# Output projection of a hybrid layer: conv half as seven block products, quarter-wide weight scales, sums held in PSUM

## The chip, the cores and the metric

One core of a Trainium2 chip runs the kernel. Its engines work side by side, each through its own instruction stream in order: TensorE (PE) multiplies into PSUM, VectorE (DVE) and ScalarE (ACT) read PSUM and SBUF, GpSimd (POOL) works on SBUF, and SyncE's queue (SP) issues most DMA transfers. The metric is the device time of one execution in microseconds; the result is given as the median of repeated runs. TensorE's clock has two levels, 1.2 and 2.4 GHz; the profile shows what share of full speed was granted.

## The reference, cut to what matters

For 512 tokens of width 2048 the layer computes an SSD group and a conv group, joins them to a row of 4096 and projects that row back:

```python
mixed = jnp.concatenate([y_ssd, y_conv], axis=-1)            # (1, 512, 4096)
h = h + jnp.einsum('ble,ed->bld', mixed, w_out)              # w_out (4096, 2048), float32
return rmsnorm(h, final_norm_w)
```

`y_conv = silu(layernorm(conv31(glu))) * silu(cg)` is the half that the change computes in another way. All inputs and the output are float32.

## The kernel before, in words

**Numbers.** Each float32 operand is scaled by a power of two and split into two float16 parts, hi and lo. A product is three matmuls (hi by hi, hi by lo, lo by hi; `mm`, line 388). A weight tile of 128x2048 floats (1 MB, buffer `raw`, three of them) is prepared by `prepare` (line 406): ACT squares it with a running sum, a 1-column matmul on PE adds that sum over the partitions into one column of the PSUM tile `pk` (`total`, line 366), DVE and POOL make the scale and its inverse from the exponent (`scales`, line 373), ACT writes hi (`w_h`, four buffers), DVE writes lo (`w_l`, three buffers; `low`, line 385).

**Items.** `plan` (line 1028) lists 121 items in the order in which PE takes them: 73 of the input projection with the SSD and the 31-tap convolution behind them, 16 for the gate `cg` (`take_cg`, line 893), and 32 of the output projection. The layer norm's sums over the channels (`center`, line 870, and `normalize`, line 885) hang on two items of the last SSD groups. An output item is a quarter `d` of the 2048 output columns (512 wide) by a block `p` of 512 of the 4096 inputs: `p` 0 to 3 is the SSD half (`mixh`, `mixl`), 4 to 7 the conv half (`z`, `y` or `cc`). It takes 4 token tiles of 128 x 4 input tiles of 128 x 3 = 48 matmuls with 512 moving columns (`project_out`, line 929, `out_tile`, line 942). After every item DVE adds its four PSUM tiles, scaled, to the result rows in SBUF (`take_out`, line 987; the rows are called `big`, as they lie where the layer's input was, and start with `x`). The conv half is split into hi and lo by `split_conv` (line 912) in the gate stage, with a scale for each block of 512 channels. The last three items of the last quarter are taken token tile by token tile, so that a row can be finished and stored while the next is multiplied (`project_last`, line 948; `finish`, line 1011).

**Order.** Nothing is issued in the order in which it is written. `Program` records every instruction with a cost from a small table (`Engine.cost`, line 249), gives it a due time from PE's order and simulates the engines (`times`, line 179, `AHEAD_NS` = 4000 early for what feeds the main matmuls); each engine then gets its stream in the simulated order. The 1-column matmuls are taken as soon as the simulation has their input. On the chip each stream is fixed: an instruction that waits holds up all behind it. All instructions carry the helper's line 284 in the profile, so groups are told apart by their tiles.

**PSUM.** Eight banks of 128x512 floats: `pp` three, `ps` three, `pst` and `pk` one each.

Of the kernel before, what the change touches and what calls it, by code (L numbers as in the profile page):

```python
# [40 lines left out]
SPLIT_AT = 2  # L41
# [5 lines left out]
N_LAST = 3  # L47
# [263 lines left out]
class Kernel:  # L311
    def __init__(self, ctx, tc, t, out):
        self.ctx, self.tc, self.t, self.out = ctx, tc, t, out
        self.program = Program()
        self.nc = Engines(self.program, tc.nc)
        self.v = self.nc.vector
        pool = self.pool
        self.const = pool("const", 1)
        self.raw = pool("raw", 3)
        self.wsp = pool("wsp", 3)  # L320
        self.big = pool("big", 1)
        self.mix = pool("mix", 1)
        self.ccp = pool("ccp", 4)
        self.wk = pool("wk", 1)
        self.tiny = pool("tiny", 4)
        self.pp = pool("pp", 3, space=PSUM)
        self.ps = pool("ps", 3, space=PSUM)
        self.pst = pool("pst", 1, space=PSUM)
        self.pk = pool("pk", 1, space=PSUM)
        self.dram = pool("dram", 1, space=DRAM)  # L330


    def pool(self, name, bufs, **kw):
        pool = self.ctx.enter_context(self.tc.tile_pool(name=name, bufs=bufs, **kw))
        return Pool(self.program, pool, name, bufs, kw.get("space") is not None)

# [29 lines left out]
    def total(self, x):  # L366

        self.n_totals += 1
        ps = self.pk_tile[:, self.n_totals - 1:self.n_totals]
        self.nc.tensor.matmul(ps, self.ones16, x.bitcast(BF16)[:, 1:2], start=True, stop=True)  # L370
        return ps

    def scales(self, m, bound=0, keep=None):


        g = self.nc.gpsimd
        e = self.small("sc_e", 1, I32)
        self.v.tensor_scalar(e, m.bitcast(I32), 1, 0x7F800000, op0=ALU.logical_shift_right, op1=ALU.bitwise_and)
        sc = self.const.tile([P, 1], I32, name=keep + "_s") if keep else self.small("sc_s", 1, I32)
        self.v.tensor_scalar(sc, e, -1.0, float((205 - bound) << 23), op0=ALU.mult, op1=ALU.add)  # L380
        inv = self.const.tile([P, 1], I32, name=keep) if keep else self.small("sc_i", 1, I32)
        g.tensor_scalar(inv, e, 1.0, float((49 + bound) << 23), op0=ALU.mult, op1=ALU.add)
        return sc.bitcast(F32), inv.bitcast(F32)
# [22 lines left out]
    def prepare(self, it, pieces=1):  # L406
        if "raw" not in it:
            self.load(it)
        his, sqs, los = [], [], []
        for k, w in enumerate(it["raw"]):  # L410
            hi = self.wsp.tile([P, 2048], F16, name="w_h", bufs=4)[:, :w.shape[1]]
            s = self.small(f"sq{k}")
            self.nc.scalar.activation(hi.bitcast(BF16), w, AF.Square, accum_out=s)
            his.append(hi)
            sqs.append(s)
        if len(sqs) > 1:
            self.nc.gpsimd.tensor_tensor(sqs[0], sqs[0], sqs[1], op=ALU.add)
        it["sc"], it["inv"] = self.scales(self.total(sqs[0]))
        for w, hi in zip(it["raw"], his):
            lo = self.wsp.tile([P, 2048], F16, name="w_l", bufs=3)[:, :w.shape[1]]  # L420
# [27 lines left out]
    def constants(self):  # L448
        nc, t, c = self.nc, self.t, self.const
        self.pk_tile, self.n_totals = self.pk.tile([P, 512], F32, name="pk"), 0  # L450
        self.ones, self.ident = (c.tile([P, P], F32, name=name) for name in ("ones", "ident"))
# [459 lines left out]

    def split_conv(self, p):
# [11 lines left out]
        nc.scalar.activation(hi, self.cc[p], AF.Copy, scale=sc)  # L924
        self.low(lo, self.cc[p], sc, hi)
        self.mixed[4 + p] = Split(hi, lo, inv)


    def project_out(self, d, p):
        def go(it):  # L930
            if d == 0 and p == 0:
                self.start_output()
            pool, name = ((self.pp, "pp"), (self.ps, "ps"))[p % 2]
            it["ps"] = []
            for i in range(TT):
                ps = pool.tile([P, S], F32, name=name) if i < 3 else self.pst.tile([P, S], F32, name="pst")
                self.out_tile(ps, it, p, i)
                it["ps"].append(ps)

        return go  # L940

    def out_tile(self, ps, it, p, i, first=0):

        m, w, n = self.mixed[p], it["parts"][0], ps.shape[1]
        at = lambda k: k * S + i * P if p >= 4 else k // 2 * TT * GC + i * GC + k % 2 * P
        self.mm(ps, [(m.cols(at(k), at(k) + P), w.cols(k * S + first, k * S + first + n)) for k in range(4)])

    def project_last(self, it):

        d, its = 3, list(enumerate(self.items))[-N_LAST:]  # L950
        its = [(x, n - len(self.items) + 8) for n, x in its]
        scs = [self.out_scale(x, p) for x, p in its]
        for i in range(TT):
            for (x, p), sc in zip(its, scs):
                parts = N_PARTS if i == TT - 1 and p == 7 else 1
                w = S // parts
                for q in range(parts):
                    pool, name = ((self.pp, "pp"), (self.ps, "ps"))[(p + q) % 2]
                    ps = pool.tile([P, S], F32, name=name)[:, :w]
                    self.out_tile(ps, x, p, i, q * w)  # L960
                    row = self.row(i)[:, d * S + q * w:d * S + (q + 1) * w]
                    self.v.scalar_tensor_tensor(row, ps, sc, row, op0=ALU.mult, op1=ALU.add)
                    if p == 7:
                        self.square(row, self.oss[:, i, d + q:d + q + 1])
            self.finish(i, parts)

    def out_scale(self, it, p):
        sc = self.small("inv0")
        self.nc.gpsimd.tensor_tensor(sc, it["inv"], self.mixed[p].inv, op=ALU.mult)
        return sc  # L970
# [15 lines left out]

    def take_out(self, d, p):
        def take(it):
            nc, v = self.nc, self.v
            ds = slice(d * S, (d + 1) * S)  # L990
            sc = self.out_scale(it, p)
            if d == 0 and p == 7:
                self.fw = self.ccp.tile([P, D], F32, name="cc")
                nc.gpsimd.dma_start(self.fw, self.t["final_norm_w"].partition_broadcast(P))
            for i in range(TT):
                row = self.row(i)[:, ds]
                v.scalar_tensor_tensor(row, it["ps"][i], sc, row, op0=ALU.mult, op1=ALU.add)
                if p == 7:
                    self.square(row, self.oss[:, i, d:d + 1])
            if d > 0 and p == 0:  # L1000
                for i in range(TT):
                    row = self.row(i)[:, (d - 1) * S:d * S]
                    v.tensor_tensor(row, row, self.fw[:, (d - 1) * S:d * S], op=ALU.mult)
            if d == 3 and p == 0:
                self.part = self.const.tile([P, TT], F32, name="part")
                v.tensor_tensor(self.part, self.oss[:, :, 0], self.oss[:, :, 1], op=ALU.add)
                v.tensor_tensor(self.part, self.part, self.oss[:, :, 2], op=ALU.add)
                v.tensor_scalar(self.part, self.part, 1.0 / D, EPS, op0=ALU.mult, op1=ALU.add)
        return take
# [18 lines left out]
    def plan(self):  # L1028
# [27 lines left out]
        for ct in range(KT):  # L1056
            add(blk(64 + ct), self.project, self.take_cg(ct))
        for p in range(4):
            self.later.append((len(items) - 13 + 4 * p + SPLIT_AT, p))
        for d in range(4):  # L1060
            for p in range(8):
                if 8 * d + p < 32 - N_LAST:
                    add([t["w_o"][d, p]], self.project_out(d, p), self.take_out(d, p))
                else:
                    add([t["w_o"][d, p]], self.project_last if p == 7 else lambda it: None)
        for i, p in self.later:
            items[i]["takes"].append(lambda it, p=p: self.split_conv(p))
        self.items = items

    def run(self):  # L1070
# [7 lines left out]
        self.conv_sums = self.const.tile([P, 4, 5], F32, name="conv_sums")  # L1078
        for i, it in enumerate(self.items):
            if i > 0:  # L1080
                self.prepare(it)
# [13 lines left out]
def _layout(inp):  # L1095
# [15 lines left out]
    lay["w_o"] = c(o.transpose(3, 0, 2, 1, 4).reshape(4, 8, P, 4 * S))  # L1111
# [30 lines left out]
```

## Time and profile before

| | |
|---|---|
| time before, median of 3 runs | 1454.96 us (1454.14 to 1455.84) |
| the profiled execution | 1456.17 us, its span 1454.4 us |
| PE busy | 1421.3 us, 98% of the span |
| DVE, ACT, POOL busy | 1131.6 us (78%), 810.3 us (56%), 213.7 us (15%) |
| the chain that ended last | PE 88%, DVE 7%, ACT 2%, DMA 1% |
| output projection on PE | about 1109 to 1444 us |

The profile is of one execution; the span is the time in which its engines had work, and 1.8 us of the execution lie around it. Busy time counts an engine as busy while any of its instructions is in flight; matmuls overlap, so a matmul that is listed with 379 ns follows the one before it by much less, and what one costs is read from the starts of neighbours in the order of time. An engine's idle time is named after what ended it. The chain of waits goes back from the last instruction to whatever released it.

### The profile page before, as it was taken

The numbers are of one execution on the slowest core, as the hardware profiler recorded it, in microseconds if no ns is written. First come the engines' busy times: TensorE is split into PE (matmuls) and PEld (weight loads), VectorE is DVE, ScalarE is ACT, GpSimd is POOL, SyncE is SP. The second block draws the span as 40 slices with busy tenths as digits, with TensorE's granted clock in tenths as the row PEclk, the third lists the DMA queues.
The fourth block names the chain that finished last, engine by engine and source line by source line (L and its number), as shares of the span: only waits on it lengthen the run. The fifth ranks groups of instructions, "written<-read, shape, count | busy, mean of one in ns | idle before, by whom it ended". The sixth has DMA issues, their size and how long they took to land.

```text
span 1454.4 us, 20437 instructions
## 1 busy us (share of the span) xinstructions
PE 1421.3 (98%) x7857; PEld 767.4 (53%) x7857; DVE 1131.6 (78%) x1897; ACT 810.3 (56%) x1162; POOL 213.7 (15%) x375
## 2 busy tenths in 40 slices
PE   7999999999999999999999979999999999999997
PEld 5544475456456547547575465754444444444443
DVE  6899998997997997897886998985455554555555
ACT  7654456456656556556557558677665443444432
POOL 2224221211110111101000162101100000000001
PEclk9999999999999999999999999999999999999998
DMA  6332323343342343343344324333326332323203
GB/s 245 128 129 88 127 96 122 109 130 104 118 135 101 116 117 122 113 121 114 101 115 143 108 80 143 100 125 102 116 87 232 116 116 87 113 90 105 98 29 116
DMA packets 83233, 169.32 MB, mean 116 GB/s; under 512 B 45872, under 2 KB 63360, under 8 KB 66368
## 3 DMA queue, kind: packets, MB, share of 16 engines
q1 hardware_dynamic: 82048, 164.71, 34.2%
q10 hardware_dynamic: 720, 2.10, 0.4%
q8 instruction: 61, 1.00, 0.3%
q0 software_dynamic: 368, 1.21, 0.2%
q14 instruction: 36, 0.29, 0.1%
HBM read 153.78 MB, written 4.26 MB: 109 GB/s over the span
## 4 chain that ended last, share of the span: by engine, by line
PE 88%; DVE 7%; ACT 2%; DMA 1%; issue 1%; POOL 1%; SPq 0%; DVEq 0%; ACTq 0%; POOLq 0%
PE pp L284 70%; PE ps L284 13%; PE pst L284 5%; DVE cc L284 3%; DVE w_l L284 1%; ACT w_h L284 1%; DMA cc<-in_x 1%; PE pk L284 0%; DVE y L284 0%; ACT big L284 0%; DMA cumb<-cum_rows 0%; DVE x L284 0%; ACT mixh L284 0%; POOL sq L284 0%; POOL mu L284 0%
## 5 line engine op out<-in xcount | busy, mean ns | idle before, releaser
L284 PE MATMUL pp<-big,w_h 128*128 128x512 f16 (+1 forms) x2592 | 778.5, 377 | 0.5 <-ACT big L284 0.3
L284 PE MATMUL pp<-big,w_l 128*128 128x512 f16 (+1 forms) x1296 | 488.0, 377 | 0.0
L284 PEld LDWEIGHTS <-w_h 128*128 128x128 f16 x2592 | 256.0, 99 | 279.7 <-issue 4.8
L284 DVE SCALAR_TENSOR_TENSOR w_l<-raw,sc_s,w_h 128x2048 f16<-128x2048 f32 (+1 forms) x132 | 301.9, 2287 | 111.6 <-PE pst L284 41.1
L284 ACT ACTIVATE w_h<-raw 128x2048 bf16<-128x2048 f32 x129 | 244.7, 1897 | 212.8 <-PE pst L284 111.3
L284 DVE SCALAR_TENSOR_TENSOR cc<-glu,taps,cc 128x503 f32<-128x503 f32 (+24 forms) x480 | 345.5, 740 | 5.7 <-ACT cc L284 2.6
L284 ACT ACTIVATE w_h<-raw,sc_s 128x2048 f16<-128x2048 f32 (+1 forms) x132 | 256.0, 1950 | 105.5 <-DVE sc_s L284 97.8
L284 PEld LDWEIGHTS <-w_l 128*128 128x128 f16 x1296 | 128.6, 99 | 147.4 <-issue 10.9
L284 PE MATMUL pp<-w_h,big 128*128 128x256 f16 (+1 forms) x1152 | 176.7, 262 | 0.0
L284 POOL TENSOR_SCALAR sc_i<-sc_e 128x1 int32<-128x1 int32 x121 | 45.1, 373 | 889.9 <-DVE sc_e L284 792.6
L284 PEld LDWEIGHTS <-big 128*128 128x128 f16 x1728 | 155.2, 98 | 26.7 <-issue 7.1
L284 PE MATMUL pp<-w_l,big 128*128 128x256 f16 (+1 forms) x576 | 145.8, 262 | 0.0
L284 PEld LDWEIGHTS <-cc 128*128 128x128 f16 x588 | 56.8, 98 | 66.9 <-issue 1.9
L284 PEld LDWEIGHTS <-mixh 128*128 128x128 f16 x512 | 49.9, 98 | 61.5 <-issue 3.2
L284 DVE SCALAR_TENSOR_TENSOR big<-pp,inv,big 128x512 f32<-128x512 f32 (+1 forms) x50 | 37.2, 745 | 48.9 <-PE pp L284 47.8
L284 DVE SCALAR_TENSOR_TENSOR big<-ps,inv,big 128x512 f32<-128x512 f32 (+1 forms) x50 | 37.2, 744 | 43.4 <-PE ps L284 43.3
L284 ACT ACTIVATE m<-cumb,cum 128x128 f32<-128x128 f32 x128 | 42.1, 389 | 38.2 <-PE ps L284 35.7
L284 PE MATMUL ps<-w_h,cc 128*128 128x512 f16 (+1 forms) x208 | 62.6, 375 | 0.0
L284 ACT ACTIVATE th<-pp,inv 128x512 f32<-128x512 f32 x32 | 21.9, 683 | 62.6 <-PE pp L284 62.6
L284 PEld LDWEIGHTS ps<-xdt,m 128*128 128x128 f32 x256 | 42.6, 194 | 7.1 <-DVE m L284 1.3
L284 POOL TENSOR_TENSOR mu<-mu,cc 128x512 f32<-128x512 f32 x15 | 29.5, 1969 | 91.2 <-DVE cc L284 91.2
L284 PEld LDWEIGHTS <-mixl 128*128 128x128 f16 x256 | 25.0, 98 | 28.7 <-issue 0.5
(213 smaller groups left out, 1652.4 us busy)
## 6 DMA issues: line engine op xcount, KB each, us to landing
raw<-in_w_blk SPq DMA_DIRECT2D x80, 1024.0 KB, 4.9
raw<-in_w_o SPq DMA_DIRECT2D x32, 1024.0 KB, 4.9
raw<-in_w_z SPq DMA_DIRECT2D x16, 1024.0 KB, 4.9
cumb<-cum_rows SPq DMA_DIRECT2D x32, 256.0 KB, 3.4
big<-in_x SPq DMA_DIRECT2D x4, 768.0 KB, 9.2
cc<-in_x SPq DMA_DIRECT2D x4, 512.0 KB, 5.8
cc<-in_x SPq DMA_DIRECT2D x2, 1024.0 KB, 12.8
out<-big SPq DMA_DIRECT2D x3, 512.0 KB, 2.6
```

The lines of the kernel that those rows point to most:

```text
L284: self.program.add(self.kind, lambda: op(*args, **kw), self.cost(name, outs, ins, kw.get("transpose", False)), moved, outs, ins, kw.get("s ...
```

## The change

The conv half of a quarter is the product of a 512 x 2048 matrix (tokens by channels) and a 2048 x 512 one, summed over four channel blocks `p`. The changed kernel cuts tokens, channels of a block and columns in half each, so that the product of two by two blocks takes seven block products in place of eight: `split_conv` builds the four sums and differences of the token and channel halves (`s1` to `s4`), `prepare_seven` those of the weight's blocks (`t`), and `project_seven` does seven products of 12 matmuls with 256 moving columns for each of the two token tiles of a half: 84 matmuls for an item. The products `q1` to `q7` stay in seven PSUM banks over all four `p`; `take_core` and `take_corners` combine and add them to the rows once a quarter.

The SSD half of quarters 1 and 2 and one of its blocks in quarter 3 are added to the same banks (`project_joint`, 96 matmuls with 256 columns; the eighth bank takes the corner that has no product of its own). Quarter 0's SSD half comes first of all and is summed in four banks (`project_own`, 48 matmuls with 512 columns, taken once); the last three items, now SSD blocks 1 to 3 of quarter 3, are done as before. All conv channels share one scale (`conv_scale`), and each quarter of the weights has one: the squares are summed ahead by `sum_squares`, which loads every weight tile of the output a second time: 8 times in the SSD stage (every sixth item from item 24), once an item in the gate stage (ACT and DVE in turn), once in each of the first 8 output items. `split_conv` moves from the gate stage to the first four output items. The load of `final_norm_w` moves from POOL's queue to SP's, and the memory kept for POOL's DMA descriptors falls to 4096 bytes of a partition.

```diff
-SPLIT_AT = 2
-N_LAST = 3
+ORDER = (0, 1, 2, 3)
+OUT = ((1, (0, 1, 2, 3, 4, 5, 6, 7)), (2, (4, 0, 5, 1, 6, 2, 7, 3)), (0, (4, 5, 6, 7)), (3, (4, 0, 5, 6, 7)))
+LAST = (1, 2, 3)
+FIRST_SQUARES = 24
+SEVEN = (("q1", "m11", 0), ("q6", "s2", 5), ("q7", "s3", 4), ("q5", "s1", 3), ("q2", "m12", 2), ("q4", "m22", 6), ("q3", "s4", 1))
+BANKS = (("q1", "pp"), ("q6", "ps"), ("q7", "pp"), ("q5", "ps"), ("q2", "pp"), ("q4", "ps"), ("q3", "pst"), ("q8", "pk"))
...
-        self.wsp = pool("wsp", 3)
+        self.wsp = pool("wsp", 4)
+        self.wtp = pool("wtp", 1)
...
     def split_conv(self, p):
-        ssq = self.conv_sums[:, p, 4:5]
-        v.tensor_reduce(ssq, self.conv_sums[:, p, :4], op=ALU.add, axis=mybir.AxisListType.X)
-        sc, inv = self.scales(self.total(ssq), 0, f"conv_{p}")
+        s3, s2, s4 = (self.th() for _ in range(3))
+        v.tensor_tensor(kn(s3), m11, m21, op=ALU.subtract)
+        v.tensor_tensor(m21, m22, m21, op=ALU.subtract)
+        v.tensor_tensor(kn(s2), m11, m21, op=ALU.add)
+        v.tensor_tensor(kn(s4), m12, kn(s2), op=ALU.subtract)
...
+        for (name, y), (tag, bufs) in zip((("s3", s3), ("s2", s2), ("s4", s4)), FORM_ROOM[p]):
+            nc.scalar.activation(f[:, :S], y, AF.Copy, scale=self.c_scale)
+            self.low(f[:, S:], y, self.c_scale, f[:, :S])
...
+    def sum_squares(self, d, n, on_act):
+            w = self.raw.tile([P, 2048], F32, name="raw")
+            self.nc.sync.dma_start(w, self.t["w_o"][d, n] if n < 4 else self.t["w_s"][d, n - 4])
+            if on_act:
+                self.nc.scalar.activation(junk, w, AF.Square, accum_out=to)
+            else:
+                self.v.scalar_tensor_tensor(junk, w, 1.0, w, op0=ALU.mult, op1=ALU.mult, accum_out=to)
+            if n == 7:
+                self.v.tensor_reduce(s, self.w_sums, op=ALU.add, axis=mybir.AxisListType.X)
+                self.w_scales[d] = self.scales(self.total(s, bank), 1, f"wo{d}")
...
+    def prepare_seven(self, d):
+            t = self.wtp.tile([P, 2, 4, H], F32, name="wt")
+            v.tensor_tensor(t[:, :, 0:2], w[:, :, 0:2], w[:, :, 3:4].broadcast_to([P, 2, 2, H]), op=ALU.add)
+            v.tensor_tensor(t[:, :, 2], t[:, :, 0], w[:, :, 1], op=ALU.add)
+            v.tensor_tensor(t[:, :, 3], t[:, :, 2], w[:, :, 2], op=ALU.add)
+            for k in range(2):
+                self.nc.scalar.activation(hi[:, :3 * H], fn(w[:, k, :3]), AF.Copy, scale=sc)
+            for k in range(2):
+                self.nc.scalar.activation(his[k][:, 3 * H:7 * H], fn(t[:, k]), AF.Copy, scale=sc)
+            for k in range(2):
+                self.low(los[k][:, :3 * H], fn(w[:, k, :3]), sc, his[k][:, :3 * H])
+            for k in range(2):
+                self.low(los[k][:, 3 * H:7 * H], fn(t[:, k]), sc, his[k][:, 3 * H:7 * H])
...
+    def project_seven(self, d, p, last, closes):
+            for name, f, b in SEVEN:
+                for i in range(2):
+                    for k, (hi, lo) in enumerate(it["seven"]):
+                        l = tuple(x[:, i * P:(i + 1) * P] for x in self.forms[p - 4, f, k])
+                        pairs.append((l, (hi[:, b * H:(b + 1) * H], lo[:, b * H:(b + 1) * H])))
+                    self.add_to(d, name, i, pairs, last and (name in CORE or closes))
...
+    def take_core(self, d):
+            self.nc.scalar.copy(q1, q["q1"])
+            v.tensor_tensor(a, q["q6"], q1, op=ALU.subtract)
+            add(0, 0, q1, inv)
+            v.tensor_tensor(b, a, q["q7"], op=ALU.subtract)
+            add(1, 0, b, self.minus[d])
+            v.tensor_tensor(a, a, q["q5"], op=ALU.subtract)
+            v.tensor_tensor(b, b, q["q5"], op=ALU.subtract)
+            add(0, 1, a, inv)
+            add(1, 1, b, inv)
...
+    def take_corners(self, d):
+            for name, h, e in (("q2", 0, 0), ("q4", 1, 0), ("q3", 0, 1), ("q8", 1, 1)):
+                    v.scalar_tensor_tensor(to, q[name].rearrange("p (t n) -> p t n", t=2), inv, to, op0=ALU.mult, op1=ALU.add)
+            if d == 3:
+                return
...
+                self.nc.sync.dma_start(self.fw, self.t["final_norm_w"].partition_broadcast(P))
+            for i in range(TT):
+                self.square(row, self.oss[:, i, d:d + 1])
+                v.tensor_tensor(row, row, self.fw[:, d * S:(d + 1) * S], op=ALU.mult)
...
-    nc = bacc.Bacc("TRN2", target_bir_lowering=False, num_devices=1)
+    nc = bacc.Bacc("TRN2", target_bir_lowering=False, num_devices=1, dynamic_dma_scratch_size=4096)
```

## Rows read from the trace of the kernel before

**Rows 1.** The page, part 1: busy time, share of the span, instructions of each engine.

```profile
PE 1421.3 (98%) x7857; PEld 767.4 (53%) x7857; DVE 1131.6 (78%) x1897; ACT 810.3 (56%) x1162; POOL 213.7 (15%) x375
```

**Rows 2.** Busy times by stretch: layer norm's sums, gate, output; columns in the first line.

```profile
core 0: us, PE busy (x) PEld busy (x) DVE busy (x) ACT busy (x) POOL busy (x), PEclk, DMA share, GB/s
840.00:900.00 60.00, 52.36 (x320) 34.96 (x319) 54.30 (x72) 42.92 (x85) 28.95 (x24) 0.94 0.28 81
941.00:1109.00 168.00, 168.00 (x815) 80.35 (x814) 97.49 (x155) 111.16 (x161) 20.38 (x45) 1.00 0.32 106
1109.00:1445.00 336.00, 335.20 (x1580) 151.70 (x1578) 188.51 (x274) 135.57 (x127) 17.59 (x65) 1.00 0.30 110
```

**Rows 3.** PE's waits: total us, times, longest, whole span; the longest two groups.

```profile
PE pk L284 <- ACT w_h L284: 8.1, 3, 5.2
PE pst L284 <- ACT mixh L284: 6.1, 1, 6.1
```

**Rows 4.** PE in order of time, an output item: start, duration, what, count.

```profile
1122.05 0.38 PE L284 MATMUL ps<-w_l,mixh 128*128 128x512 f16 x1
...
1132.19 0.38 PE L284 MATMUL pp<-w_h,mixh 128*128 128x512 f16 x1
1132.51 0.16 PE L284 MATMUL pk<-sq,ones 128*128 128x1 bf16 x1
1132.53 0.38 PE L284 MATMUL pp<-w_l,mixh 128*128 128x512 f16 x1
```

**Rows 5.** PE in order of time, an SSD item with 256 columns, and a stall.

```profile
839.81 0.27 PE L284 MATMUL pp<-w_l,big 128*128 128x256 f16 x1
...
854.22 0.27 PE L284 MATMUL pp<-w_l,big 128*128 128x256 f16 x1
859.69 0.16 PE L284 MATMUL pk<-sq,ones 128*128 128x1 bf16 x1 [5.20 <-ACT w_h L284]
```

**Rows 6.** The page, part 5: weight loads of the SSD items; busy us, mean ns.

```profile
L284 PEld LDWEIGHTS <-big 128*128 128x128 f16 x1728 | 155.2, 98 | 26.7 <-issue 7.1
```

**Rows 7.** DVE in order of time, first output items.

```profile
1121.47 0.74 DVE L284 SCALAR_TENSOR_TENSOR big<-pp,inv,big 128x512 f32<-128x512 f32 x1
1122.12 2.34 DVE L284 SCALAR_TENSOR_TENSOR w_l<-raw,sc_s,w_h 128x2048 f16<-128x2048 f32 x1
1124.38 0.74 DVE L284 SCALAR_TENSOR_TENSOR big<-ps,inv,big 128x512 f32<-128x512 f32 x1
```

**Rows 8.** ACT in order of time, first output items.

```profile
1116.14 3.88 ACT L284 ACTIVATE w_h<-raw,sc_s 128x2048 f16<-128x2048 f32 x2
1119.97 1.91 ACT L284 ACTIVATE w_h<-raw 128x2048 bf16<-128x2048 f32 x1
1121.79 0.19 ACT L284 ACTIVATION_READ_ACCUMULATOR w_h<-raw 128x1 f32 x1
```

**Rows 9.** DMA: a weight tile's median time to landing (last column).

```profile
raw<-in_w_o SPq DMA_DIRECT2D x32, 1024.0 KB, 4.9
```

**Rows 10.** Busiest DMA stretch; last columns are DMA share and GB/s.

```profile
1120.00:1125.00 5.00, 5.00 (x25) 2.25 (x24) 5.00 (x5) 1.98 (x3) 0.00 (x0) 1.00 1.03 426
```

**Rows 11.** SP's own waits: total us, times, longest; the longest group.

```profile
SPq L284 <- DVE w_l L284: 787.0, 105, 18.1
```

**Rows 12.** DVE and ACT in order of time around the stall of Rows 5.

```profile
852.39 9.65 DVE L284 TENSOR_TENSOR cc<-cc,mu 128x512 f32<-128x512 f32 x7
...
857.65 1.89 ACT L284 ACTIVATE w_h<-raw 128x2048 bf16<-128x2048 f32 x1
```

**Rows 13.** DVE groups by form: the subtraction of the mean; busy, mean ns.

```profile
L284 DVE TENSOR_TENSOR cc<-cc,mu 128x512 f32<-128x512 f32 x16 | 18.4, 1185 | 0.0
```

**Rows 14.** POOL in order of time at the start.

```profile
6.08 0.56 POOL L284 DMA_DIRECT2D c_ln_b<-in_ln_b  x1
11.39 0.33 POOL L284 TENSOR_SCALAR nw_w<-c_norm_w,nw_s 128x16 f32<-128x16 f32 x1 [4.75 <-DVE nw_s L284]
```

**Rows 15.** DMA: the last of POOL's seven loads at the start; us to landing.

```profile
c_ln_b<-in_ln_b POOLq DMA_DIRECT2D x1, 8.0 KB, 6.6
```

More of the change, by code (lines that the diff above doesn't have):

```diff
@@ L923, in split_conv @@
             hi, lo = both[:, :4 * S], both[:, 4 * S:]
[L924 to L929, printed above, removed]
-        def go(it):
-            if d == 0 and p == 0:
+        nc.scalar.activation(hi, self.cc[p], AF.Copy, scale=self.c_scale)
+        self.low(lo, self.cc[p], self.c_scale, hi)
+        at = {"m11": 0, "s1": 1, "m12": 2, "m22": 3}
+        for name, j in at.items():
+            for k in range(2):
+                a = (4 * k + j) * H
+                self.forms[p, name, k] = (hi[:, a:a + H], lo[:, a:a + H])
@@ new lines, in joint_scale, with own_scale @@
+    def joint_scale(self, d):
+        if d not in self.joint:
+            sc, inv = self.col(), self.col()
+            self.v.tensor_scalar_mul(sc, self.w_scales[d][0], self.less)
+            self.v.tensor_scalar_mul(inv, self.w_scales[d][1], self.c_inv)
+            self.joint[d] = sc, inv
+        return self.joint[d]
+    def own_scale(self, d):
+        if d not in self.own:
+            self.own[d] = self.col()
+            self.v.tensor_scalar_mul(self.own[d], self.w_scales[d][1], self.y_inv)
+        return self.own[d]
@@ new lines, in sums, with add_to @@
+    def sums(self, d):
+        if d not in self.banks:
+            pools = {"pp": self.pp, "ps": self.ps, "pst": self.pst, "pk": self.pk}
+            self.banks[d] = {n: pools[tag].tile([P, S], F32, name=tag) for n, tag in BANKS}
+            self.begun[d] = set()
+        return self.banks[d]
+    def add_to(self, d, name, i, pairs, last):
+        bank, n = self.sums(d)[name], len(pairs)
+        for x, (l, r) in enumerate(pairs):
+            for j, (a, b) in enumerate(((l[0], r[0]), (l[0], r[1]), (l[1], r[0]))):
+                start = name not in self.begun[d]
+                self.begun[d].add(name)
+                self.nc.tensor.matmul(bank[:, i * H:(i + 1) * H], a, b, start=start,
+                                      stop=last and i == 1 and x == n - 1 and j == 2)
@@ L940, in project_out, with take_own, take @@
[L940 to L946 removed]
+                self.out_tile(self.plain[i], it, p, i, p == 0, p == 3)
+        return go
+    def take_own(self, d):
+        def take(it):
+            inv = self.own_scale(d)
+            for i in range(TT):
+                row = self.row(i)[:, d * S:(d + 1) * S]
+                self.v.scalar_tensor_tensor(row, self.plain[i], inv, row, op0=ALU.mult, op1=ALU.add)
+        return take
@@ new lines, in out_tile @@
+    def out_tile(self, ps, it, p, i, start=True, stop=True, first=0):
+        m, w, n = self.mixed[p], it["parts"][0], ps.shape[1]
+        at = lambda k: k // 2 * TT * GC + i * GC + k % 2 * P
+        for k in range(4):
+            (l, r) = m.cols(at(k), at(k) + P), w.cols(k * S + first, k * S + first + n)
+            for j, (a, b) in enumerate(((l[0], r[0]), (l[0], r[1]), (l[1], r[0]))):
+                self.nc.tensor.matmul(ps, a, b, start=start and k == 0 and j == 0, stop=stop and k == 3 and j == 2)
@@ L948, in project_last @@
     def project_last(self, it):
-        d, its = 3, list(enumerate(self.items))[-N_LAST:]
-        its = [(x, n - len(self.items) + 8) for n, x in its]
-        scs = [self.out_scale(x, p) for x, p in its]
+        d, its, sc = 3, list(zip(self.items[-N_LAST:], LAST)), self.own_scale(3)
         for i in range(TT):
-            for (x, p), sc in zip(its, scs):
-                parts = N_PARTS if i == TT - 1 and p == 7 else 1
+            for n, (x, p) in enumerate(its):
+                ends = n == N_LAST - 1
+                parts = N_PARTS if i == TT - 1 and ends else 1
@@ L985, in row @@
         return self.acc[i // 2][:, i % 2, :]
[L987 to L1009, printed above, removed]
     def finish(self, i, parts):
```

171 lines of the change are left out of this document (142 added, 29 removed).

## The prediction, made before the change was run

> **What bounds the kernel now.** I read the page's busy shares first: PE is busy for 1421.3 of 1454.4 us, DVE for 78% [rows 1]. As a share is a mean over stages, I went on to the busy times by stretch: in the gate stage PE has no idle time, in the 336 us of the output projection 0.8 us, while DVE is busy there for 188.5 and ACT for 135.6 us [rows 2]. The reader is to see that the stage which the change rewrites is bound by PE alone; a matmul less there is time less, until another engine takes its place. The list of PE's waits holds one thing more: its longest stalls are at the start and at a 1-column matmul that waits for ACT [rows 3]; the latter lies in the layer norm's stretch, where PE is busy for 52.4 of 60 us at a mean granted clock of 0.94 [rows 2].
>
> **What a matmul costs.** Matmuls overlap, so I take the spacing of their starts. In an output item 47 steps take 10.14 us: 215.7 ns for one with 512 columns. The same place in the next item comes after 10.48 us, 48 x 0.2157 = 10.35 of it matmuls; the remaining 0.125 us is the 1-column matmul of the weight's scale [rows 4]. Matmuls with 256 columns stand in the SSD items: 132 steps from 839.81 to 854.22, 109.2 ns each [rows 5]. That is 1.3 ns more than half. A weight load, needed before each, is 98 ns long [rows 6] and is hidden in both.
>
> At this the Trainium skill speaks against the change: "TensorE: Matmul & The Clock Gate", section "Back-to-back issue gap", says that in a stream of weight loads and matmuls the spacing is set by both, and gives about 131 ns for 512 columns and 81 ns for 128, so that a narrow matmul is dear for its columns. By it (an estimate from that page: some 98 ns for 256) the half-width products would cost three quarters of the full ones and the change would lose. The rows show 215.7 and 109.2 ns, so here the rule doesn't hold.
>
> **The change on PE.** Before: 32 items x 48 = 1536 full matmuls, 331.3 us. After: 16 conv items x 84 and 9 joint items x 96 = 2208 half matmuls, 241.1 us, and 7 plain items x 48 = 336 full ones, 72.5 us; together 313.6. Gain 17.7 us: a conv item falls from 10.35 to 9.17, a joint item rises to 10.48. The 1-column matmuls fall from 36 (32 items, 4 conv blocks) to 5 (4 quarters, 1 for conv): 31 x 0.125 = 3.9 us. Sum: 21.6 us.
>
> **DVE, the next engine.** Neighbours start 0.65 us apart for 512 elements and 2.26 us for 2048 [rows 7], so some 0.13 us and 1.04 ns an element: 0.93 us for 768, 1.20 for 1024. I use this for additions without a scalar too. A conv item then costs 1.20 + 2 x 0.66 for the sums and 2 x 0.93 + 2 x 1.20 for lo, 6.8 us in all; the core of a quarter 8 x 0.66 = 5.3, its corners 2.0 to 2.6, squares and final weight of the rows 4 x 0.66 = 2.6. Quarters 1 and 2 (4 plain lo, 4 conv items, the rest) need 46.8 us of DVE in 78.6 us of PE. Quarter 0 has nothing but its four conv items: 4 x 6.8 + 5.3 + 2.0 + 2.6 = 37.1 us of DVE in 4 x 9.17 = 36.7 of PE. From the end of quarter 2's last conv item to the plain item in quarter 3, PE takes 10.48 + 36.7 + 9.17 + 10.48 = 66.8 us and DVE has about 63.5 us to do. So DVE just fits, at 95%, with no room for its own waits for ACT's hi. ACT itself needs some 3.5 us for a conv item's hi, from 1.9 us for 2048 elements [rows 8], and fits. I take 1.5 us of PE waits here, between 0 and 12 (DVE idle for a fifth of that stretch: 63.5/0.8 - 66.8).
>
> **Banks.** All eight are held by one quarter, so PE's first product of a quarter waits for the core of the one before. A product takes 12 x 0.109 = 1.31 us. `q1`, `q6`, `q7`, `q5` end at 1.3 to 5.2 us of the last item's 9.2, the core has read them by about 7.2, and they are wanted again at 9.2, 10.5, 11.8 and 13.1; `q2` at 14.4. DVE may thus be 5 us late, two plain lo's worth, before PE waits; what stands in its queue there is the next items' lo. I take 0. The end is alike: the last plain item's third hi buffer comes free only with the last conv item; ACT 1.9 and DVE 2.3 us [rows 7, 8] with their gaps make 4.6, PE wants it after two products of 12 x 0.2157 = 5.2. I take 0.5, between 0 and 4.7 (the rest of the core ahead of it). The tail from there is unchanged.
>
> **The squares, moved ahead.** 32 more loads of 1 MB. One lands in 4.9 us [rows 9]; the gate stage will ask for 2 MB in 10.48 us, 200 GB/s, where 426 has been moved [rows 10]. Its DVE rises from 97.5 to about 116 and its ACT (2.1 us a square with the read-out [rows 8]) from 111 to about 128 of 168 us. Nothing there is late; uncovered, one load would cost its 4.9 us. `split_conv` adds 6.9 us of DVE to each of the first four output items, beside 2.3: 9.2 of 10.4, and its results are wanted only 80 us after the first; 0. The joint scale and the rows of `x` are wanted 40 us later than they are ready; 0.
>
> The 8 squares in the SSD stage are the doubtful part. Each is 2.1 us of ACT and takes one of three `raw` buffers, so the next loads wait at SP's head for it, and the 31-tap weights, the SSD's rows and its transposes wait behind them. SP waits 105 times for such a buffer, 7.5 us in the mean [rows 11], and PE hardly feels it outside the layer norm's sums. There it does: DVE's seven subtractions stretch over 9.65 us [rows 12], as one takes 1185 ns in the mean [rows 13] and not some 660; ACT's squares queue behind them, and PE has a 1-column matmul in its stream that needs ACT's [rows 5, 12]. One of the eight squares (item 66) lands here, and the sum over quarter 0's eight adds a 1-column matmul. Its price lies between -7.6 (the planner's new order undoes the stall) and +5.2 (a second one as long); I take +1.
>
> **POOL and SP.** POOL's seven loads at the start are issued by 6.6 us and its next work at 11.39 waits 4.75 for DVE [rows 14]: 4.75 us of waiting for descriptor memory cost nothing. If the smaller memory held one load at a time, 7 x 6.6 us [rows 15] would hold POOL till 46 and PE's start with it, some 35 us. Loads of 8 KB make that unlikely. The final weight's load stands in SP's queue in quarter 1, 30 us ahead of its use; 0.
>
> **Sum.** The profiled execution was 1456.2 (span and 1.8 around it): 1456.2 - 21.6 + 3.0 = 1437.6. The runs' median is 1.2 below that execution: 1436.4, say 1436.
>
> **Rivals and chances.** About 0.2% (3 us) is what a measurement can tell from no change.
> - *Forecast*, 0.60: PE still ends last, waits of 0 to 7 us in the output stage and the SSD together: 1433 to 1440.
> - *DVE becomes the bound* in quarter 0 and at its seams, or the last item waits, 0.15: 7 to 12 us of the gain are lost, 1440 to 1446. For it 95% of DVE on paper; against it the two conv items that can be prepared ahead.
> - *A second stall* of 5 to 8 us in the SSD stage, 0.05: 1441 to 1446.
> - *The old stall goes* with the new order, 0.12: 1428 to 1433.
> - *Slower: the banks.* If PE finds DVE behind at every seam, the whole unloading lies bare: 8 instructions of the core, 4 corners and ACT's copy, 12 x 0.66 + 0.6 = 8.5 us at four seams, 34 us: 1467 to 1470. It decides from 21.6/4 = 5.4 us a seam. For it the full PSUM; against it the order of the products and 5 us of room. 0.03. POOL's start (above) would end there too, 1470: 0.01.
> - *Half width costs more than half*: from (241.1 + 21.6)/2208 = 119 ns on, nothing is gained; with the weight load bare, 98 + 109 ns, the time would be 1650. That is the way in which the Trainium skill's rule above would turn it. Only one row bears on it, and it says 109.2. 0.01.
> - *The change doesn't do what it says*, as another engine sets the output stage's pace at 10.4 us an item: 1453 to 1457, 0.03.
>
> Faster 0.92, same 0.03, slower 0.05. The range leaves out the slower cases, no change, and part of the two ends: 1429 to 1446.
>
> **What would show it.** Right: in the profile after, the output stage lasts about 314 to 317 us in place of 336, PE without idle time; the conv matmuls stand 109 ns apart, 84 to an item; some 970 more matmuls in all; PE waits for `pp` or `ps` under 3 us. Wrong: PE waits for DVE `w_l` in quarter 0 (first rival), for DVE at the first `q1` or `q2` of a quarter (banks), a spacing above 112 ns, a longer stall than 5.2 us by 860 us, or POOL's first scale after 12 us.

## The result and the profile after

The changed kernel takes 1431.36 us (median, 1430.84 to 1431.85) beside 1455.38 us for the kernel before in the same series: a ratio of 0.9836, 95% interval 0.9819 to 0.9853, a gain of 24.0 us. The forecast was 1436 us with a range of 1429 to 1446. The profiled execution of after took 1431.85 us, its span is 1430.1 us.

Page, part 1, of after (busy us, share of the span, instructions):

```profile
PE 1401.6 (98%) x8834; PEld 865.7 (61%) x8834; DVE 1187.1 (83%) x1929; ACT 829.5 (58%) x1210; POOL 218.4 (15%) x311
```

Beside [rows 1], PE has 977 matmuls more and is busy for 19.7 us less; DVE has 55.5 us more to do. Busy times by stretch, after: layer norm's sums, gate stage, output stage, quarter 0's four conv items, and the tight stretch from quarter 2 to quarter 3 (columns in the first line):

```profile
core 0: us, PE busy (x) PEld busy (x) DVE busy (x) ACT busy (x) POOL busy (x), PEclk, DMA share, GB/s
840.00:900.00 60.00, 54.51 (x320) 34.92 (x319) 53.55 (x72) 42.03 (x85) 27.80 (x24) 0.94 0.29 92
941.00:1106.00 165.00, 164.43 (x787) 77.58 (x786) 108.41 (x160) 115.57 (x162) 26.15 (x38) 1.00 0.57 209
1106.00:1420.00 314.00, 313.91 (x2560) 250.07 (x2558) 226.69 (x290) 130.25 (x145) 4.19 (x5) 1.00 0.36 133
1313.20:1349.90 36.70, 36.70 (x339) 32.89 (x337) 30.05 (x33) 17.02 (x22) 0.00 (x0) 1.00 0.29 103
1294.90:1361.70 66.80, 66.80 (x615) 59.87 (x613) 57.31 (x69) 31.09 (x42) 0.00 (x0) 1.00 0.31 111
```

The output stage is still PE's alone, as in [rows 2]: PE is without work for 0.09 of its 314 us. Where the gain lies is read from the stage's first and last matmul, in the order of time on PE. Before:

```profile
1108.94 0.38 PE L284 MATMUL pp<-w_h,mixh 128*128 128x512 f16 x1
...
1444.16 0.27 PE L284 MATMUL pp<-w_h,cc 128*128 128x256 f16 x1
```

After:

```profile
1106.29 0.38 PE L292 MATMUL pp<-w_h,mixh 128*128 128x512 f16 x1
...
1314.40 0.27 PE L292 MATMUL pp<-w_h,cc 128*128 128x256 f16 x1
...
1323.57 0.27 PE L292 MATMUL pp<-w_h,cc 128*128 128x256 f16 x1
...
1420.07 0.27 PE L292 MATMUL ps<-w_h,mixl 128*128 128x256 f16 x1
```

From first to last start the stage takes 335.22 us before and 313.78 after: 21.44 us less. It begins 2.65 us sooner, and what follows the last matmul is 0.21 us shorter (10.24 and 10.03 us up to the span's end). Together 24.30, beside 24.32 between the two profiled executions (1456.17 and 1431.85). The middle lines are the first matmul of `q1` in two conv items that follow each other: 9.17 us for 84 matmuls, 109.2 ns each.

The sooner start is the sum of two parts with opposite signs. Up to the output stage PE runs the same main matmuls in the same order in both kernels, so that one and the same matmul can be compared; here the one that sums the squares of the layer norm over the channels, before and then after:

```profile
913.87 1.02 PE L284 MATMUL pst<-glu,ones 128*128 128x512 f32 x2
909.75 1.02 PE L292 MATMUL pst<-glu,ones 128*128 128x512 f32 x2
```

Up to there after is 4.12 us ahead. From there to the first matmul of the output stage, which is the end of the SSD stage and the whole gate stage, before takes 195.07 us and after 196.54: it gives 1.47 us back.

PE's waits over the whole span of after (total us, times, longest); none of them lies in the output stage:

```profile
PE pst L292 <- ACT mixh L292: 6.0, 1, 6.0
PE pk L292 <- ACT w_h L292: 5.9, 3, 3.1
PE pp L292 <- DVE m L292: 2.1, 2, 1.7
PE pk L292 <- POOL sq L292: 2.0, 4, 0.8
```

The second line is the group of [rows 3] that was 8.1 us with a longest wait of 5.2. DVE in the order of time in quarter 0, the place that was feared, shows why PE has no wait there:

```profile
1315.24 1.95 DVE L292 SCALAR_TENSOR_TENSOR w_l<-raw,kept,w_h 128x768 f16<-128x768 f32 x2 [2.40 <-ACT w_h L292]
1317.11 2.48 DVE L292 SCALAR_TENSOR_TENSOR w_l<-wt,kept,w_h 128x1024 f16<-128x1024 f32 x2
1319.62 1.23 DVE L292 TENSOR_TENSOR wt<-raw 128x1024 f32<-128x1024 f32 x1
1320.88 1.42 DVE L292 TENSOR_TENSOR wt<-wt,raw 128x512 f32<-128x512 f32 x2
1324.41 1.95 DVE L292 SCALAR_TENSOR_TENSOR w_l<-raw,kept,w_h 128x768 f16<-128x768 f32 x2 [2.11 <-ACT w_h L292]
```

A conv item keeps DVE for 7.1 us (6.8 by the prediction), then DVE is idle for 2.1 to 2.4 us until ACT's next hi. The items repeat every 9.17 us: DVE follows PE's pace and doesn't set it. (ACT isn't the bound either: before each of these items' hi it has been idle for 5.3 to 5.5 us.)

### The profile page after: what moved, and what is told of

It reads as the page before. It is cut to its first block, busy times and chain, and to the rows that moved or that the text cites. A ratio compares the mean times of both kernels' runs of the same rounds, so it can differ in the third digit from the quotient of the medians.

```text
span 1430.1 us, 22425 instructions
## 1 busy us (share of the span) xinstructions
PE 1401.6 (98%) x8834; PEld 865.7 (61%) x8834; DVE 1187.1 (83%) x1929; ACT 829.5 (58%) x1210; POOL 218.4 (15%) x311
## 4 chain that ended last, share of the span: by engine, by line
PE 85%; DVE 9%; ACT 2%; issue 2%; DMA 1%; POOL 0%; SPq 0%; DVEq 0%; ACTq 0%
PE pp L292 68%; PE ps L292 12%; PE pst L292 3%; DVE cc L292 3%; PE pk L292 2%; DVE w_l L292 2%; ACT w_h L292 1%; DMA raw<-in_w_s 1%; DVE th L292 1%; DVE y L292 1%; DMA cc<-in_x 1%; ACT big L292 0%; DVE x L292 0%; DVE bT L292 0%; DMA bt<-th 0%
## 5 line engine op out<-in xcount | busy, mean ns | idle before, releaser
L292 DVE SCALAR_TENSOR_TENSOR cc<-glu,taps,cc 128x511 f32<-128x511 f32 (+21 forms) x480 | 345.3, 744 | 3.0
L292 DVE SCALAR_TENSOR_TENSOR w_l<-raw,sc_s,w_h 128x2048 f16<-128x2048 f32 (+1 forms) x100 | 228.0, 2284 | 20.3 <-ACT w_h L292 20.2
L292 ACT ACTIVATE w_h<-raw 128x2048 bf16<-128x2048 f32 x97 | 183.6, 1893 | 104.4 <-PE pp L292 100.7
L292 ACT ACTIVATE w_h<-raw,sc_s 128x2048 f16<-128x2048 f32 (+1 forms) x100 | 192.5, 1934 | 46.3 <-DVE sc_s L292 39.7
L292 ACT ACTIVATE w_h<-raw,kept 128x768 f16<-128x768 f32 (+1 forms) x48 | 60.8, 1285 | 136.0 <-issue 58.7
L292 POOL TENSOR_SCALAR sc_i<-sc_e 128x1 int32<-128x1 int32 x90 | 34.6, 384 | 655.6 <-DVE sc_e L292 587.8
L292 DVE SCALAR_TENSOR_TENSOR w_l<-raw,kept,w_h 128x768 f16<-128x768 f32 (+1 forms) x48 | 69.4, 1460 | 74.2 <-ACT w_h L292 74.0
L292 PEld LDWEIGHTS <-mixh 128*128 128x128 f16 x808 | 79.0, 98 | 32.6 <-issue 0.4
L292 ACT ACTIVATE raw<-raw 128x2048 bf16<-128x2048 f32 x24 | 45.6, 1901 | 15.8 <-DMA raw<-in_w_o 8.7
L292 PEld LDWEIGHTS <-mixl 128*128 128x128 f16 x404 | 39.5, 98 | 16.0
```

What stands on the lines that cost most here:

```text
L292: self.program.add(self.kind, lambda: op(*args, **kw), self.cost(name, outs, ins, kw.get("transpose", False)), moved, outs, ins, kw.get("s ...
```

## Experiments

All are shown with the output stage's length from the first to the last start of a matmul in their own profile. Before is 1454.86 us in the series of the first four experiments and 1455.4 to 1455.8 in those of the others. A stage length repeats to 0.2 us between profiles of kernels with the same stage (before, e4 and e8; after, e3 and e10). A beginning is that of a single execution and is good to some 3 us only: the profiled one of e3 took 1434.56 us beside its median of 1431.25, that of e4 1450.24 beside 1452.17.

| kernel | median, us | ratio to before (95%) | stage begins | stage, us |
|---|---|---|---|---|
| before | 1455.38 | | 1108.94 | 335.22 |
| after | 1431.36 | 0.9836 (0.9819 to 0.9853) | 1106.29 | 313.78 |
| e1_eight_products | 1453.76 | 0.9993 (0.9984 to 1.0003) | 1106.18 | 335.25 |
| e2_before_one_scale | 1451.97 | 0.9981 (0.9972 to 0.9990) | 1108.83 | 331.97 |
| e3_no_ssd_squares | 1431.25 | 0.9843 (0.9829 to 0.9856) | 1109.05 | 313.78 |
| e4_before_lo4 | 1452.17 | 0.9980 (0.9971 to 0.9988) | 1103.16 | 335.14 |
| e8_before_scratch | 1455.66 | 0.9999 (0.9990 to 1.0007) | 1108.69 | 335.01 |
| e5_dve_plus2 | 1434.41 | 0.9851 (0.9836 to 0.9866) | 1107.74 | 314.85 |
| e6_dve_plus4 | 1458.77 | 1.0023 (1.0014 to 1.0032) | 1107.86 | 339.23 |
| e7_core_plus16 | 1462.70 | 1.0053 (1.0039 to 1.0066) | 1105.89 | 344.15 |
| e7_core_plus8 | 1453.91 | 0.9993 (0.9984 to 1.0003) | 1105.79 | 335.77 |
| e10_core_plus8_behind | 1431.80 | 0.9838 (0.9822 to 0.9854) | 1106.52 | 313.78 |

**Eight products on the changed frame.** After, with the conv items done as joint items (the eighth product's bank used by all) and the weights' conv blocks as they were. The part of the edit in `plan`:

```diff
-                if p < 4:
-                    out(d, p, self.prepare_plain(d, True), self.project_joint(d, p, closes, p == plain), *takes)
-                else:
-                    out(d, p, self.prepare_seven(d), self.project_seven(d, p, p == seven, closes), *takes)
+                out(d, p, self.prepare_plain(d, p < 4), self.project_joint(d, p, closes, closes), *takes)
```

> The changed kernel with the conv half as eight block products: quarter-wide weight scales, squares ahead, sums kept in PSUM and the order of the items stay; a conv item is 96 half-width matmuls in place of 84, without sums of blocks and without the core. Theory (PE alone sets the output stage): 16 x 12 x 0.109 = 21.0 us more than the changed kernel, 1452.3, some 3 us below the kernel before, output stage 335 us. Rival (the gain comes from fewer evictions and 1-column matmuls, not from the seventh product): 1432 to 1440.

The stage is 21.47 us longer than after's, as 16 items with 12 more matmuls of 109.2 ns give (21.0). It is as long as before's to 0.03 us: 29 1-column matmuls less in the stage (31 before, 2 here; the other two of the forecast's 31 lay in the gate stage) are worth 3.5 us by the next run's 0.12 us each, but 25 items with 96 matmuls of 109.2 ns cost 3.2 us more than 25 with 48 of 215.7, and 0.6 us go to one wait. So seven products in place of eight carry the whole gain of the stage; the frame around them is even there. The time, 1453.76 us, is 1.5 us above the theory's 1452.3 and far from the rival's 1432 to 1440.

**One scale in the kernel before.** A quarter's later items take the scale of its first.

```diff
...
+        if "like" in it:
+            it["sc"], it["inv"] = it["like"]["sc"], it["like"]["inv"]
+        else:
+            it["sc"], it["inv"] = self.scales(self.total(sqs[0]), 0, it.get("keep"))
...
```

> The kernel before, but each output item takes the weight scale of the first item of its quarter: 28 of the 36 one-column matmuls, with their squares, go; nothing else. Theory (each of them costs 0.125 us of PE): 28 x 0.125 = 3.5 us less than before, 1451.9, an output item 10.35 us. Rival (they are hidden, or their place is taken by a wait for lo): 1455, items stay at 10.48.

The stage falls by 3.25 us, and 27 of the 28 1-column matmuls that go lie in it: 0.12 us each; [rows 4] gave 0.125.

**No squares in the SSD stage.** The first quarter's eight squares are left out; its scale is that of the next quarter.

```diff
+                self.w_scales.setdefault(0, self.w_scales[d])
...
-        squares = [(d, n) for d in ORDER for n in range(8)]
-        for i in range(8):
-            items[FIRST_SQUARES + 6 * i]["takes"].append(self.sum_squares(*squares.pop(0), True))
+        squares = [(d, n) for d in ORDER[1:] for n in range(8)]
```

> The changed kernel without the eight squares in the SSD stage (quarter 0 takes quarter 1's scale). For the 2.65 us by which the changed kernel is ahead when the output stage begins. Theory A (the extra loads and squares put the planner's order otherwise, and so shorten the waits by accident): most of it is lost, 1433 to 1434. Theory B (it is from something else, such as the fourth lo buffer): 1431.4 within 0.7, output stage beginning at 1106 as in the changed kernel. If the squares cost something there after all: 1429 to 1431.

No difference clear of the noise: the medians, of four runs each, are 0.1 us apart, while this kernel's runs reach from 1430.32 to 1434.56. So nothing speaks for the squares having brought the 2.65 us; a cost of 1 us is too small to be told here. The stage of the profiled execution begins at 1109.05, not at the theory's 1106: that execution has PE waits for ACT of 4.07 us at 865.6 and 1.89 us at 940.6 where after's has 2.38 and 0.38.

**A fourth lo buffer in the kernel before, and the descriptor memory alone.**

```diff
-        self.wsp = pool("wsp", 3)
+        self.wsp = pool("wsp", 4)
...
-            lo = self.wsp.tile([P, 2048], F16, name="w_l", bufs=3)[:, :w.shape[1]]
+            lo = self.wsp.tile([P, 2048], F16, name="w_l", bufs=4)[:, :w.shape[1]]
...
-    nc = bacc.Bacc("TRN2", target_bir_lowering=False, num_devices=1)
+    nc = bacc.Bacc("TRN2", target_bir_lowering=False, num_devices=1, dynamic_dma_scratch_size=4096)
```

> The kernel before with four lo buffers in place of three and 4096 bytes of descriptor memory, nothing else. Theory B (the fourth buffer lets weights be ready sooner in the SSD stage): output stage begins 1 to 2.6 us sooner, 1452.8 to 1454.4. Theory A (the squares' loads changed the order): 1455.4 within 0.7. If the small descriptor memory held POOL up, its first scale at the start would come after 12 us and the time would rise.

The second kernel has only the last of these edits:

> The kernel before with 4096 bytes of descriptor memory alone, without the fourth lo buffer. Separates the two edits of the run before it that gave 2.7 us. If the fourth lo buffer does it: 1454.9 within 0.7, output stage beginning near 1108.9. If the descriptor memory does it (or where buffers come to lie): 1452.2.

The buffer brings 2.7 us of the median (1.7 to 4.2 by the interval) and the descriptor memory nothing. What the buffer does is read from DVE's waits ahead of `w_l` (total us, times, longest), first with three buffers (the kernel with the smaller descriptor memory):

```profile
DVE w_l L284 <- PE pst L284: 41.1, 25, 1.7
DVE w_l L284 <- PE pp L284: 32.7, 20, 5.9
```

then with four, the only line of `w_l` among the longest:

```profile
DVE w_l L284 <- ACT w_h L284: 60.0, 51, 1.8
```

With three, DVE waits 45 times for PE, which has to give a lo buffer back first; with four it waits for ACT's hi alone. Behind that, PE's waits for the sums of squares fall as they do in after (8.1 to 6.0, longest 5.2 to 3.1; and 3.9 to 1.6):

```profile
PE pk L284 <- ACT w_h L284: 6.0, 4, 3.1
PE pk L284 <- POOL sq L284: 1.6, 3, 0.8
```

In this kernel's profile the matmul that sums the layer norm's squares comes at 907.87, 6.00 us sooner than before's. Some 1.8 us of that are TensorE's clock (an estimate, 0.03 of 60 us): from 840 to 900 us the granted clock is 0.97 here and 0.94 in before and in after:

```profile
840.00:900.00 60.00, 54.52 (x327) 34.29 (x326) 54.58 (x75) 43.58 (x86) 27.83 (x24) 0.97 0.30 95
```

The 4.2 us that are left are about what after gains up to there (4.12). From there to the output stage this kernel takes 195.29 us. All four profiles of the kernel before and its variants lie between 194.96 and 195.29, all eight of after and its variants between 196.04 and 197.86, the one without the eight squares too (197.86). So the 1.47 us that after gives back belong to its frame and not to the buffer or those eight squares. After's PE has waits of 0.38 and 0.46 us in this stretch, before's none; a kernel without the squares and loads of the gate stage, the likely cause, was not run.

**How much DVE time was left.** In after, the weight's first sum is done three times, then five times, in each conv item: 2.3 and 4.6 us more of DVE.

```diff
...
+            for _ in range(5):
-            v.tensor_tensor(t[:, :, 0:2], w[:, :, 0:2], w[:, :, 3:4].broadcast_to([P, 2, 2, H]), op=ALU.add)
+                v.tensor_tensor(t[:, :, 0:2], w[:, :, 0:2], w[:, :, 3:4].broadcast_to([P, 2, 2, H]), op=ALU.add)
```

> The changed kernel with the first of the three sums of weight blocks done three times in each conv item: 2.3 us more of DVE an item, the same result. In the changed kernel DVE was busy for 57.3 of the 66.8 us around quarter 0, in which five conv items are prepared, so it has 1.9 us an item to spare. Theory (PE binds with some 2 us an item of room on DVE): 0 to 2 us more, 1431 to 1433.5. Rival (DVE fits with no room, as the prediction had it, 95% on paper): every conv item of quarters 0 and 3 waits, 1438 or more.

> The same with five times: 4.6 us more of DVE an item. Theory: DVE now needs 57.3 + 5 x 4.6 = 80 us around quarter 0 where PE needs 66.8, so 13 us are lost there and 4 to 8 more where quarter 1's conv items run into quarter 2's: 1445 to 1453; PE waits for the hi and lo of conv items. Rival (preparing ahead covers it): 1432 to 1436.

With 2.3 us more an item, PE waits 0.75 us in the whole stage, and the median is 3.0 us above after's (the runs reach from 1430.78 to 1435.99), 0.9 above the theory's range; of the 2.5 us between the two profiled spans 1.07 lie in the stage and 1.45 ahead of it. With 4.6 us it is 27.4 us above, beyond the theory's range too and slower than the kernel before. PE's waits in the stage of that run, the first three of five groups that sum to 16.5 us:

```profile
PE ps L292 <- ACT w_h L292: 7.3, 3, 4.8
PE pp L292 <- DVE w_l L292: 3.0, 1, 3.0
PE ps L292 <- DVE w_l L292: 2.3, 4, 1.1
```

So the first rival's mechanism is there, some 2 to 4 us of DVE an item away. Its price is above what the sum of DVE's work gives: the stage is 25.4 us longer for 16.5 us of waits. The rest is told with the next run.

**How late the core may be.** In after, the core's first subtraction, which reads the banks of `q6` and `q1`'s copy, is done 17 and then 9 times: 9.8 and 4.9 us more for each of four cores.

```diff
+            for _ in range(9):
-            v.tensor_tensor(a, q["q6"], q1, op=ALU.subtract)
+                v.tensor_tensor(a, q["q6"], q1, op=ALU.subtract)
```

> The changed kernel with the core's first subtraction done 17 times: 16 x 0.61 = 9.8 us more of DVE between the end of the second product and the freeing of the third and fourth bank of a quarter, the same result. Theory (5 us of room at a seam): about 4 to 5 us lost where conv items meet conv items (quarters 1 to 2 and 0 to 3), less at the other two: 1438 to 1446, with PE waiting for DVE at pp or ps. Rival 1 (a seam has no room): 4 x 9.8, 1470. Rival 2 (room of 10 us or more): 1431 to 1433.

> The kernel after with eight more copies of one 0.61 us VectorE subtraction in each quarter's core, 4.9 us more for each of four cores (the value is the same). Three seams lie inside the output stage. Theory as predicted (5 us of room at a seam): every core still fits, 1431 to 1435 us, with less than 2 us of TensorE waits for pp or ps in the stage. Rival (room of about 2 us only, as 2.3 us an item was free and 4.6 was not): 3 us of wait at each of two or three seams, with the slow matmuls behind a stall (the granted clock of 0.68 to 0.89 in the stretches that hold one in the run with 9.8 us more) adding up to 2 us each: 1438 to 1446 us.

Both times are above the theory's, and the smaller step's, 1453.91, is above the rival's too: it eats nearly the whole gain. PE in the order of time at the seam behind quarter 1, with 4.9 us more:

```profile
1228.93 0.27 PE L292 MATMUL pp<-w_h,cc 128*128 128x256 f16 x1 [1.33 <-ACT w_h L292]
1233.44 0.40 PE L292 MATMUL ps<-w_h,x 128*128 128x256 f16 x1 [4.24 <-DVE th L292]
...
1236.61 0.42 PE L292 MATMUL pp<-w_h,x 128*128 128x256 f16 x1
1236.83 0.42 PE L292 MATMUL pp<-w_l,x 128*128 128x256 f16 x1
...
1238.71 0.27 PE L292 MATMUL ps<-w_l,z 128*128 128x256 f16 x1
1238.82 0.27 PE L292 MATMUL ps<-w_h,y 128*128 128x256 f16 x1
```

PE wants `q6`'s bank at 1229.20 and gets it 4.24 us late. Behind that the same matmuls stand 0.22 us apart, and 0.11 again by 1238.8. The granted clock shows it, here for the 10 us behind each of the three longest stalls of that run:

```profile
1233.44:1243.44 10.00, 10.00 (x71) 8.11 (x72) 9.66 (x14) 4.04 (x9) 0.00 (x0) 0.76 0.22 93
1355.13:1365.13 10.00, 10.00 (x66) 7.73 (x66) 9.93 (x15) 2.70 (x6) 0.00 (x0) 0.70 0.29 105
1410.69:1420.69 10.00, 10.00 (x35) 4.04 (x36) 8.56 (x13) 0.72 (x2) 0.47 (x1) 0.75 0.00 0
```

PE is busy throughout, yet 24, 30 and 25% of its clock are missing: 2.4 + 3.0 + 2.5 = 7.9 us. With 13.3 us of waits that makes 21.2 of the 22.0 us by which the stage is longer than after's. Of the waits 8.5 us are for a bank (4.24 and 4.29); 2.4 are for a lo of DVE's and 2.4 for hi of ACT's. The same reading gives 16.5 + 6.9 = 23.4 of 25.4 us for the run with 4.6 us an item, and 20.1 + 8.5 = 28.6 of 30.4 us for the one with 9.8 us a core.

Was DVE out of time, or was the bank held? DVE at the same seam, same run:

```profile
1219.54 1.41 DVE L292 TENSOR_TENSOR th<-ps,th 128x512 f32<-128x512 f32 x2
1220.86 1.01 DVE L292 SCALAR_TENSOR_TENSOR w_l<-raw,kept,w_h 128x768 f16<-128x768 f32 x1
...
1229.23 2.35 DVE L292 SCALAR_TENSOR_TENSOR w_l<-raw,kept,w_h 128x2048 f16<-128x2048 f32 x1
...
1232.69 0.69 DVE L292 TENSOR_TENSOR th<-ps,th 128x512 f32<-128x512 f32 x1
```

The nine reads of the bank, 5.5 us of work, are spread over 13.8 us, as DVE's fixed order puts the next items' lo and sums between them. That order, made by the planner, seems to be most of the cost: in after the core starts at 1222.61, and nine such reads in a row from there would end near 1228.1 (an estimate, 0.60 us each), where after's PE wants the bank at 1227.94. An order that keeps the nine together was not run. The last run puts the same 4.9 us behind the core, on SBUF tiles alone:

```diff
             add(1, 1, b, inv)
+            for _ in range(8):
+                v.tensor_tensor(q1, a, b, op=ALU.subtract)
```

> The kernel after with the same 4.9 us of VectorE time in each quarter's core as the run before (eight subtractions of 512 elements), but put behind the core's last addition and on SBUF tiles alone, so that no bank is held for longer (the value of the tile is not used again). Theory A (what cost 22 us was the time for which the banks are held, the extra steps being queued among the next item's lo): without it TensorE waits less than 3 us in the output stage, 1431 to 1435 us. Theory B (VectorE has no 4.9 us to give at a seam, wherever they stand: the next items' lo come late): TensorE waits for w_l or w_h, 8 to 14 us and the slow matmuls behind, 1445 to 1456 us.

1431.80 us, the same as after, and PE has no wait in the stage, though DVE works 18.7 us more in it (busy times of the stage, columns as above):

```profile
1106.00:1420.00 314.00, 313.91 (x2559) 250.02 (x2557) 245.37 (x323) 129.71 (x144) 4.53 (x5) 1.00 0.36 132
```

The first of the added steps in DVE's order:

```profile
1236.37 0.68 DVE L292 TENSOR_TENSOR th<-th 128x512 f32<-128x512 f32 x1
```

It stands behind the corners of quarter 1, the seven others later still, up to 1254: as nothing waits for them, the planner moved them out of the seam. So some 20 us of DVE cost nothing where no bank hangs on them, and 22 us of time where one does. Whether DVE could give 4.9 us between the core and the corners wasn't tried, nor whether the 4.8 us of waits for lo and hi come from the bank's delay or from DVE's load at the seam.

## Why the prediction was right, and where it was off

**PE's sum held.** The prediction put the matmuls at 17.7 us and the 1-column ones at 3.9 us, 21.6 together; the stage fell by 21.44, though two of the 31 1-column matmuls lay ahead of it. Its two unit costs come back: 109.2 ns at half width in the conv items (the 9.17 us of an item were forecast to the digit), and 0.12 us in the run with one scale in the kernel before, for 0.125. The run with eight products shows that the gain hangs on the product that is saved: with eight, the dearer half width and one wait use up what the fewer 1-column matmuls give.

**The added waits were too dear by 2 us.** I took 1.5 us for DVE in quarter 0 and 0.5 us for the last item's hi; both are 0. The stretch of 66.8 us, put at 63.5 us of DVE, holds 57.3: the core of quarter 2 is taken before it starts, and the lo of quarter 0's first conv item before that quarter. A quarter's work doesn't lie within a quarter's time. The core itself was sized well (8 steps from 1337.89 to 1343.25 in quarter 0, 5.36 us for 5.3).

**The SSD's term had the wrong sign and the wrong cause.** I took +1 us, between -7.6 and +5.2, and argued about the squares and the planner's new order; what lies before the output came out 2.65 us shorter. The run without the eight squares gives no sign that they count. The run with a fourth lo buffer in the kernel before gives 2.7 us by the medians: the step that failed is one that isn't there. The buffer stands in the diff (`wsp` 3 to 4), and the prediction has no term for it. That the buffer does the same in after is read from its trace (4.12 us up to the layer norm's end beside 4.2 in that run, and the same waits gone); after with three lo buffers was not run. The rival "the old stall goes" (1428 to 1433) gave the time that came, but only half of its mechanism: the longest wait for the sum fell from 5.2 to 3.1 us and didn't go, and it falls as far in the run with the buffer in the kernel before.

**The sum again.** Forecast gain 21.6 - 3.0 = 18.6 us. Measured in the profiles: 21.44 in the stage, 2.65 ahead of it, 0.21 at the end, 24.30. The difference of 5.7 us is 2.0 for waits that didn't come, 3.65 for the SSD's term, 0.21 for the tail, less 0.16 on PE. So the time came out below the main forecast's 1433 to 1440, inside the stated range: three terms erred to the same side, by 5.9 us in all.

**The banks.** The time is as forecast, no wait at any seam, but the figure of 5 us of room misleads. In after, `q6` is read by 1223.3 at quarter 1's seam and wanted by 1227.94, 4.6 us later, as the core's read and the next quarter's first matmul into that bank show:

```profile
1222.61 0.69 DVE L292 TENSOR_TENSOR th<-ps,th 128x512 f32<-128x512 f32 x1
1227.94 0.27 PE L292 MATMUL ps<-w_h,x 128*128 128x256 f16 x1
```

As an idle bank, the room is there. As DVE time ahead of the bank's release, in the order that the planner gives it, it isn't: 4.9 us more cost 22 us. The prediction named what stands in DVE's queue there, the next items' lo, and then counted the room as if the core came first. The slower rival was thus nearer than its 0.03 says: it was priced at 34 us from 5.4 us a seam on, and the runs show 22 us at 4.9 and 31 us at 9.8.

**The rest.** POOL's first scale starts at 10.93 us where [rows 14] had 11.39, and the smaller descriptor memory alone changes nothing: the 1470 us rival is out. The gate stage was put at 0, as nothing there was late on paper, and PE is idle for only 0.57 of 165 us there; yet between the layer norm's end and the output stage after takes 1.47 us more than before. That is nearly the +1 us that the prediction had, in another place, and which instructions cost it stays open.

## What to carry to other kernels

Where one engine is busy without a gap over a whole stage, count its instructions at the pitch read from neighbours' starts; that term can be right to 1%. Give every line of the diff a term, a buffer count too: here the one line without a term was worth 2.7 us in the kernel before, in a stage that the change otherwise hardly touches. And ask of an engine that is to do more not how much idle time it has, but what its fixed order puts ahead of the step that gives a buffer back: the same 4.9 us were free behind that step and cost 22 us before it, where the planner spread them among other work.

## What the hardware showed beside that

- A stall can cost more than its length. PE was at full granted clock (1.00) before the stalls of 2.43 to 4.29 us above; behind them the granted clock was at 0.50, which is 1.2 of 2.4 GHz, for a part of the next 10 us (means of 0.70 to 0.76; 0.50 from 1234 to 1238), and each took 2.4 to 3.0 us more from matmuls that had no wait of their own. Waits alone explain 13.3 of 22.0 us. It isn't so behind every stall: in e3's profile a wait of 3.09 us ends at 855.9 and the clock is at 1.00 from 856 to 864, and in e4's one of 2.39 us ends at 864.9 with 1.00 from 866 to 876.
- A matmul with 256 columns costs 109.2 ns in the conv items and one with 512 costs 215.7 ns in the plain ones, each with a weight load of its own. The Trainium skill, "TensorE: Matmul & The Clock Gate", section "Wait — 56ns, not 53.3ns?", gives columns over 2.4 GHz and some 2.5 ns more, 215.7 ns for 512 and, as an estimate from that page, 109.2 ns for 256; the trace agrees. The figures of the same page's section "Back-to-back issue gap", which the prediction weighed, don't hold here.
- A 1-column matmul in a full stream takes some 0.12 us (27 of them, 3.25 us), about as much as one with 256 columns.
